# Token differences moved to VectorE in the first value group, two more dense units in the grouped-query stage, and earlier query and key loads in the dilated attention

## The chip, the cores and the metric

The kernel runs on one core of one Trainium2 chip. The metric is the device time of one execution, in microseconds (us); lower is better. A core has TensorE (PE in the profile, with its weight loads as PEld), VectorE (DVE), ScalarE (ACT), GpSimd (POOL) and SyncE (SP). Each works through its own queue in order, and they wait for one another and for transfers (DMA) by semaphores. Most transfers here are issued from SP's queue, some from ACT's. An issue that has to wait holds up everything behind it in that queue.

## The reference

One encoder block on a sequence of 1024 tokens with 1024 channels. A normalised input goes through one wide projection. Its columns feed three mixers: a dilated window attention of three groups (dilations 1, 4 and 16), a grouped-query attention of eight query heads on two key heads, and a cross-attention into 256 memory tokens. Each mixer has a gate path; each is projected back to 1024 channels, multiplied with a sigmoid gate of the merge columns (`mg`), summed, projected once more, normalised and added to the input.

```python
h = rms_norm(x, g_pre[layer])
a_qkv, bq, bk, bv, mq, ga, gb, gm, mg = jnp.split(h @ w_in[layer], split_at, axis=-1)
...
ya = (oa * jax.nn.silu(ga)) @ w_br_a[layer]
yb = (ob * jax.nn.silu(gb)) @ w_br_b[layer]
ym = (om * jax.nn.silu(gm)) @ w_br_m[layer]
gates = jax.nn.sigmoid((mg + b_merge[layer]).astype(jnp.float32)).astype(dt).reshape(b, s, N_BRANCHES, d)
merged = gates[:, :, 0] * ya + gates[:, :, 1] * yb + gates[:, :, 2] * ym
out = merged @ w_out[layer]
x = x + rms_norm(out, g_post[layer])
```

## The kernel before

**Precision.** A float32 operand is split into a high part (ACT copies it to the type fp32r, line 105) and a low part (DVE subtracts, line 106). A product takes three matmuls: high by high, low by high, high by low.

**Stages.** The work runs in this order, and the order of PE's instructions is written out by hand throughout.

1. Loading the input, the projection of the grouped keys and values, two gate units, the memory keys and values.
2. Cross-attention (`m_att`, line 589), woven by `weave` (line 174) with dense units: the query projections of the grouped-query attention (`b_q`, line 431), the cross-attention's query units (`mq_unit`) and one merge gate unit. A *dense unit* (`add_unit`, `add_filler`) is one 128-column slice of the big projection computed outright: two halves of 512 tokens, 24 matmuls each, so 48. A merge gate unit's result goes through DVE and ACT and is stored to the DRAM tensor `thd`.
3. Grouped-query attention (`b_att`, line 712), woven with the merge gate units of `FILL[1:]`.
4. Value groups (line 974 on): the projection of the dilated attention's values. The first group takes 16 steps (n = 0 to 15) of 12 matmuls and is a plain product. The other two groups are one matrix product in Winograd's form of Strassen's algorithm, with seven half-size products (28 steps).
5. Pairs (`order`, line 1199 on): the remaining projection units are taken two at a time in the same form: seven products of 12 matmuls, 84 for a pair. There are 5 gate pairs, 12 query-key pairs and 10 merge gate pairs.
6. Dilated attention, 12 items of four steps (`q` = 0 to 47), with the branch projections (`y_units`) as filler between them.
7. The rest of the branch projections, then the output projection.

**The token differences.** Strassen's form needs sums and differences of token blocks: of the scaled input x with channels in halves 1 and 2 and tokens in halves 1 and 2. `token_block(k)` (line 572) loads two rows of tiles of x, scales them on ACT (line 577) and returns four closures; each subtracts on POOL (line 583) and stores the result to the DRAM tensor `tsd` from SP's queue (line 584). `m_att(h)` calls `token_block(h)` in its first round and one closure in each of the next four. The value groups load `tsd` again from step n = 19 on (`blocks_at`), and the pairs do so as well (`t_load`).

**How weave sets the order.** `weave` alternates two generators, the dense units and the attention, so that both advance in proportion to their cost. A generator yields a cost per piece; the pads `START_PAD`, `END_PAD` and the six `yield 300` in `b_att` only shift where dense matmuls are put, and issue nothing. `B_COST` is the sum of the attention's costs.

**Queues.** From the value groups up to the last branch projections the order of ACT, DVE, POOL and SP is written out by hand too, so a line of the program that comes earlier is earlier in its engine's queue. In the stages before, a scheduler orders these four engines.

**The first value group's queues.** At n = 2 to 5 each step splits one quarter of `raw1` (the last weights of the group, steps 4 to 7) on ACT and DVE. From n = 14 on, `split_at` prepares the first product of the Strassen form, which starts at n = 16. At n = 8 to 11 and 16 to 19 ACT moves finished sums out of PSUM (`v_store`).

**The dilated attention's helpers.** In item n, at step j (n = q // 4, j = q % 4), `other(n, j)` runs after the filler of that step. For every third item it handles the weighting of the previous head pair: `fetch` at j = 0 (loads the statistics), `weights` at j = 1 (three DVE operations and an exponential on ACT), `weights2` and `load(0, 1)` at j = 2 (store the weights to DRAM, load them broadcast). At j = 2 it also issues the next item's values and `qk_load(n + 2)`:

```python
elif j == 2:
    COM[p_]["weights2"]()
    COM[p_]["load"](0, 1)
if j == 2:
    if n + 1 < len(items):
        items[n + 1]["values"]()
    if n + 2 < len(items):
        qk_load(n + 2)
```

Of the kernel before, what the change touches and what calls it, by code (L numbers as in the profile page):

```python
# [8 lines left out]
F32 = mybir.dt.float32  # L9
R = mybir.dt.float32r  # L10
AF = mybir.ActivationFunctionType
OP = mybir.AluOpType
# [38 lines left out]
def block(ctx: ExitStack, tc: tile.TileContext, x, xT, memT, cst, msk, bcst, tabA, gpost,  # L51
# [52 lines left out]
    def split(dst_h, dst_l, src):  # L104
        A.activation(dst_h, src, AF.Copy)  # L105
        V.tensor_tensor(dst_l, src, dst_h.bitcast(F32), op=OP.subtract)  # L106
# [462 lines left out]

    half = [slice(0, 512), slice(512, 1024)]  # L570

    def token_block(k):

        x1, x2 = [mt_.tile([P, S], F32, name=f"tx{j}", bufs=1) for j in range(2)]
        for j, t in enumerate((x1, x2)):
            nc.sync.dma_start(t, xT[k + 4 * j])
            A.activation(t, t, AF.Copy, scale=cs[:, C_GP + k + 4 * j:C_GP + k + 4 * j + 1])
        (b11, b12), (b21, b22) = [[t[:, h] for h in half] for t in (x1, x2)]
        T = [mt_.tile([P, 512], F32, name=f"tb{j}", bufs=1) for j in range(4)]

        def sub(j, x, y):
            def fn():
                G.tensor_tensor(T[j], x, y, op=OP.subtract)
                nc.sync.dma_start(tsd[j, k], T[j])
            return fn

        return [sub(0, b12, b11), sub(2, b22, b12), sub(1, b22, T[0]), sub(3, b21, T[1])]

    def m_att(h):
        qh, ql = MQ[h]  # L590
        for _ in range(4):
            yield 250
        st = {}

        def scores(n):
            sv = pss1().rearrange("p (t k) -> p t k", t=2)
            nm = mt_.tile([P, 2], F32, name="mnm", bufs=3)
            l = mt_.tile([P, 2], F32, name="mls", bufs=3)
            pm = mt_.tile([P, 2, 256], F32, name="pm", bufs=2)
            for j in range(2):  # L600
                t = slice((2 * n + j) * 128, (2 * n + j) * 128 + 128)
                passes(sv[:, j], [(qh[:, t], kmh[:, h]), (qh[:, t], kml[:, h]), (ql[:, t], kmh[:, h])])
            V.tensor_reduce(nm, sv, axis=AX.X, op=OP.min)
            V.tensor_tensor(nm, nm, rcol[:, 2 * n:2 * n + 2], op=OP.mult)
            for j in range(2):
                A.activation(pm[:, j], sv[:, j], AF.Exp, scale=nrcol[:, 2 * n + j:2 * n + j + 1], bias=nm[:, j:j + 1],
                             accum_out=l[:, j:j + 1])
            rl = mt_.tile([P, 2], F32, name="mrl", bufs=4)
            V.reciprocal(rl, l)
            for j in range(2):  # L610
                V.tensor_scalar(pm[:, j], pm[:, j], rl[:, j:j + 1], None, op0=OP.mult)
            st[n] = pm

        def trans(n):
            pm = st[n]
            tp = pst().rearrange("p (k t) q -> p k t q", k=2)
            for kt in range(2):
                for j in range(2):
                    PE.transpose(tp[:, kt, j, :], pm[:, j, kt * 128:kt * 128 + 128], ident)
            ph = mt_.tile([P, 2, 256], R, name="mph", bufs=2)  # L620
            pl = mt_.tile([P, 2, 256], R, name="mpl", bufs=2)
            split(ph, pl, tp.rearrange("p k t q -> p k (t q)"))
            st[n] = (ph, pl)

        def pv(n):
            ph, pl = st.pop(n)
            o = pso()
            terms = []
            for kt in range(2):
                terms += [(vmh[:, kt, h], ph[:, kt]), (vmh[:, kt, h], pl[:, kt]), (vml[:, kt, h], ph[:, kt])]  # L630
            passes(o[:, 0:256], terms)
            om = mt_.tile([P, 256], F32, name="om", bufs=2)
            A.activation(om, o[:, 0:256], AF.Copy)
            nc.sync.dma_start(od[2, h, :, n * 256:n * 256 + 256], om)

        for n in range(7):
            if n == 0:
                blocks = token_block(h)
            elif blocks:
                blocks.pop(0)()  # L640
            if n < 4:
                scores(n)
            yield 654
            if 0 <= n - 2 < 4:
                trans(n - 2)
            yield 436
            if 0 <= n - 3 < 4:
                pv(n - 3)
            yield 654
# [36 lines left out]
    with tc.tile_pool(name="ba", bufs=1, reuse_waits="tile") as ba:  # L686
# [25 lines left out]
        def b_att():  # L712
# [63 lines left out]
            q_prep(0)  # L776
            yield 436
            for _ in range(6):
                yield 300
            for n in range(128 + LAG_F + 8):  # L780
                if n < 128:
                    i, x = divmod(n, 8)
# [22 lines left out]
                    final(m // 8)  # L805
                    yield 432

        B_COST = 128 * 1080.0 + 16 * (218 + 432 + 109) + 1800 + LAG_T * START_PAD + (LAG_F + 8) * END_PAD
        for j in FILL[1:]:
            add_filler(j)  # L810
        early[len(queue)] = first_values
# [35 lines left out]
    raw1 = t23.tile([P, 4, 512], F32, name="sum1", tag="ac3")  # L847
    for i in range(2):
        nc.sync.dma_start(raw1[:, 2 * i:2 * i + 2], wv[VG[0], :, 4 + 2 * i:6 + 2 * i])
    VR = {}  # L850
    VT = {"A11": "ac0", "A21": "ac1", "A12": "ac2", "A22": "vA22"}
    for nm, u, kh in (("A21", 1, 0), ("A11", 0, 0), ("A22", 1, 1), ("A12", 0, 1)):
# [8 lines left out]
    def parts_of(t):  # L861
        return t[:, lo], t[:, hi]
# [113 lines left out]
    for n, (i, e, k) in enumerate(steps_v):  # L976
# [12 lines left out]
        if n + 2 < 8 and n + 2 >= 4:  # L989
            v_first.append(slots0[n - 2])  # L990
            split(*parts_of(v_first[-1]), raw1[:, n - 2])
        m = n + 2 - FIRST
        if 0 <= m < 28:
            split_at(*divmod(m, 4))
# [5 lines left out]
        for nm, s0 in (("S1", 7), ("S3", 11), ("S2", 17), ("S4", 21)):  # L1000
            if 0 <= n - s0 < 4:
                sum_at(nm, n - s0)
        if n == FIRST + 10:
            for j in range(2):
                nc.sync.dma_start(tab[j], tabA[:, j])
# [307 lines left out]
    for n, nm in order:  # L1313
# [14 lines left out]
            mask = aq.tile([P, 512], F32, name="mask")  # L1328
            nc.sync.dma_start(mask, msk)
        c = n - behind_qk  # L1330
        if nm == "1" and 0 < c < 9:
            operand_store()
        if nm == "4" and 0 <= c < 8:
            operand_load(2 - c // 4, c % 4)
# [21 lines left out]
    with tc.tile_pool(name="aa", bufs=1, reuse_waits="tile") as aa:  # L1356
# [247 lines left out]

        def other(n, j):
            p_, g = divmod(n, 3)
            if g == 0 and n:
                if j == 0:
                    COM[p_] = combine(p_ - 1)
                    COM[p_]["fetch"]()  # L1610
                elif j == 1:
                    COM[p_]["weights"]()
                elif j == 2:
                    COM[p_]["weights2"]()
                    COM[p_]["load"](0, 1)
            if j == 2:
                if n + 1 < len(items):
                    items[n + 1]["values"]()
                if n + 2 < len(items):
                    qk_load(n + 2)  # L1620
            if g == 1 and p_ and j:
                c = COM[p_]
                c["weigh"](j - 1)
# [72 lines left out]
        for q in range(NQS + 2):  # L1696
# [14 lines left out]
                items[q // 4 - 1]["stats"]()  # L1711
            if q % 2 and q > 2:
                items[(q - 2) // 4]["pv"]((q - 2) % 4 // 2)
            if it:
                fill(7 if q % 2 == 0 else 5)
                other(q // 4, j)
            elif q == NQS:
                lse_turn()
                e = last_weights()
                fill(12)  # L1720
# [106 lines left out]
    end_psum()  # L1827


START_PAD, END_PAD = 700, 300  # L1830
MN_A, MN_B = 0, 7
KV_K = 5
WR, KV_STEP, RB_WAIT, KN_PAD = 2, 700, 1500, 2800.0
# [3 lines left out]
G_AT = 4  # L1837
ATT_PRIO = 120
LA_T, LA_P = 2, 3
FILL = (16, 17, 18, 19)  # L1840
GATES = ((2, 2), (2, 3), (1, 0), (1, 1), (1, 2), (1, 3), (0, 0), (0, 1), (0, 2), (0, 3))
VG = (2, 0, 1)
Y_WOVEN = 12
# [108 lines left out]
```

## Time and profile before

| What | Value |
| --- | --- |
| Median of 3 runs | 1456.14 us (1455.86 to 1456.56) |
| Profiled execution, its own time | 1459.04 us |
| Its span, first to last instruction | 1457.2 us |
| ACT busy | 660.5 us (45%) |
| POOL busy | 568.9 us (39%) |
| DMA moved | 204.26 MB, mean 140 GB/s |
| Cross-attention woven with dense units | about 98 to 231 us |
| Grouped-query attention | about 231 to 443 us |
| Value groups | 443.4 to 563.4 us |
| Pairs | 563.4 to 1086.5 us |
| Dilated attention | 1086.5 to 1317 us |
| Branch rest and output | 1317 to 1457.2 us |

How to read it. A row of a timeline is: start, duration, engine, line of the program, operation, output <- inputs, shape and count, and in brackets the idle time of that engine just before it with what ended it. A row of a stage table is: from:to, length, then for PE, PEld, DVE, ACT and POOL the busy time with the count of instructions, the granted TensorE clock as a share of full speed, the busy share of the DMA engines and what they moved in GB/s. PE is nearly always busy by its records. But the record of a matmul is longer than the time from its start to the next one's start, since matmuls are pipelined, so its busy share hides short waits; the distance from start to start (the pitch) shows them. A row of the table of waits is: engine and line that waited, what it waited for, us in total, times, the longest.

### The profile page before, as it was taken

What the parts mean: (1) busy time and instruction counts of PE and PEld (TensorE: products, weight loads), DVE (VectorE), ACT (ScalarE), POOL (GpSimd) and SP (SyncE); (2) the same over time, 40 slices, a digit from 0 to 9 for tenths busy, and PEclk for the clock granted to TensorE, in tenths of its full rate; (3) what the DMA queues carried; (4) which work ended last, traced back from release to release, by engine and by line L of the source; (5) the groups of instructions that cost most, each with busy time, mean ns of one, the idle gap of its engine ahead of it and who ended that gap; (6) DMA issues with size and microseconds to landing.
All of it is one profiled execution on the core that took longest, in us unless ns stands there. A gap on an engine that the chain in (4) does not pass through costs nothing.

```text
span 1457.2 us, 21193 instructions
## 1 busy us (share of the span) xinstructions
PE 1410.4 (97%) x7535; PEld 1118.1 (77%) x7535; DVE 940.9 (65%) x1694; ACT 660.5 (45%) x1441; POOL 568.9 (39%) x457
## 2 busy tenths in 40 slices
PE   7997998999999999999999999999999999999998
PEld 7897886555557887888888888888887777777887
DVE  7764547776742377877887877556667656867543
ACT  6554344665652345433222222444447657632221
POOL 1429502767674202323455555223300012346422
PEclk9999999999999999999999999999999999999999
DMA  6364211010005263333556565656657467637222
GB/s 239 102 201 149 77 51 44 19 33 19 19 20 185 70 219 123 138 116 100 156 164 168 164 173 166 237 196 220 205 184 244 125 200 216 212 111 260 83 96 101
DMA packets 103466, 204.26 MB, mean 140 GB/s; under 512 B 19552, under 2 KB 49472, under 8 KB 103360
## 3 DMA queue, kind: packets, MB, share of 16 engines
q1 hardware_dynamic: 89008, 188.09, 40.9%
q10 hardware_dynamic: 14352, 14.81, 2.9%
q8 instruction: 59, 0.97, 0.3%
q14 instruction: 47, 0.39, 0.1%
HBM read 134.39 MB, written 55.89 MB: 131 GB/s over the span
## 4 chain that ended last, share of the span: by engine, by line
PE 74%; DVE 7%; issue 5%; DMA 5%; POOL 4%; ACT 3%; SPq 1%; ACTq 0%; POOLq 0%; DVEq 0%
PE s L1083 34%; PE d L1287 7%; PE s L987 6%; PE sc L1799 5%; PE ov L756 3%; PE d L1494 2%; PE d L987 2%; PE s L740 1%; PE s L1431 1%; DVE bn L723 1%; PE s L741 1%; DMA ak<-qkd 1%; PE d L145 1%; PE tr L722 1%; PE d L147 1%
## 5 line engine op out<-in xcount | busy, mean ns | idle before, releaser
L1083 PE MATMUL s<-T,ch 128*128 128x512 f32 x948 | 229.5, 395 | 0.0
L1083 PEld LDWEIGHTS s<-T,ch 128*128 128x128 f32 x948 | 177.8, 188 | 42.4 <-ACT sp L1148 0.3
L106 DVE TENSOR_TENSOR ch<-sf,ch 128x512 fp32r<-128x512 f32 x106 | 92.1, 875 | 78.3 <-ACT ch L105 78.3
L747 POOL TENSOR_TENSOR bl<-bl,bp 128x512 f32<-128x512 f32 x96 | 123.3, 1284 | 39.6 <-ACT bp L743 33.0
L1083 PE MATMUL s<-hh,ch 128*128 128x512 f32 x424 | 134.9, 389 | 0.0
L1287 PE MATMUL d<-hh,wh 128*128 128x512 f32 x384 | 126.6, 399 | 1.0 <-DVE wl L1293 1.0
L1083 PEld LDWEIGHTS s<-hh,ch 128*128 128x128 f32 x424 | 79.6, 188 | 16.5
L743 ACT ACTIVATE bp<-s 128x512 f32<-128x512 f32 x128 | 75.4, 594 | 36.3 <-PE s L741 33.6
L723 DVE TENSOR_REDUCE bn<-tr 128x1 f32<-128x512 f32 x128 | 84.0, 683 | 12.1 <-PE tr L722 11.4
L1148 ACT ACTIVATE sp<-s 128x512 f32<-128x512 f32 x54 | 32.2, 596 | 128.0 <-PE s L1083 106.7
L1116 POOL TENSOR_TENSOR o<-o,rc 128x1024 f32<-128x1024 f32 x24 | 61.6, 2565 | 72.0 <-DMA o<-rs 49.9
L1083 PE MATMUL s<-hh,wl 128*128 128x512 f32 x216 | 84.3, 390 | 1.6 <-DVE wl L106 1.6
L1294 POOL TENSOR_TENSOR acc<-acc,wl 128x512 f32<-128x512 f32 x32 | 57.8, 1808 | 71.1 <-DVE wl L1293 71.1
L1287 PEld LDWEIGHTS d<-hh,wh 128*128 128x128 f32 x384 | 72.0, 188 | 16.8 <-DVE wl L1293 1.6
L1083 PE MATMUL s<-hl,wh 128*128 128x512 f32 x216 | 84.3, 390 | 0.0
L1083 PE MATMUL s<-hh,wh 128*128 128x512 f32 x216 | 84.2, 390 | 0.0
L1083 PE MATMUL s<-hl,ch 128*128 128x512 f32 x212 | 82.5, 389 | 0.0
L105 ACT ACTIVATE wh<-wr 128x1024 fp32r<-128x1024 f32 (+1 forms) x63 | 55.1, 876 | 56.6 <-DMA wr<-in_wu 13.1
L965 POOL TENSOR_TENSOR sf<-wr,sf 128x512 f32<-128x512 f32 x27 | 35.7, 1324 | 111.0 <-DVE ch L106 111.0
L1449 ACT ACTIVATE pra<-pra,sts 128x192 f32<-128x192 f32 (+2 forms) x176 | 77.4, 442 | 2.2 <-DVE sts L1441 2.2
L1287 PE MATMUL d<-hl,wh 128*128 128x512 f32 x192 | 77.7, 405 | 0.0
L1589 POOL TENSOR_TENSOR og<-og 128x1024 f32<-128x1024 f32 (+1 forms) x9 | 18.4, 2051 | 144.2 <-DVE og L1586 141.9
(397 smaller groups left out, 3662.0 us busy)
## 6 DMA issues: line engine op xcount, KB each, us to landing
wr<-in_wu SPq DMA_DIRECT2D x38, 512.0 KB, 4.6
rw<-in_wu SPq DMA_DIRECT2D x26, 512.0 KB, 4.8
o<-rs SPq DMA_DIRECT2D x96, 128.0 KB, 2.3
qkd<-o SPq DMA_DIRECT2D x24, 512.0 KB, 3.3
wl<-thd SPq DMA_DIRECT2D x24, 512.0 KB, 7.1
thd<-rs ACTq DMA_DIRECT2D x40, 256.0 KB, 3.8
aq<-qkd SPq DMA_DIRECT2D x12, 512.0 KB
ak<-qkd SPq DMA_DIRECT2D x12, 512.0 KB, 6.4
```

The costliest lines, as they stand in the source:

```text
L105: A.activation(dst_h, src, AF.Copy)
L106: V.tensor_tensor(dst_l, src, dst_h.bitcast(F32), op=OP.subtract)
L723: fp["last"] = V.tensor_reduce(st[i]["n"][:, j, c:c + 1], s, axis=AX.X, op=OP.min)
L743: A.activation(pp, s, AF.Exp, scale=-1.0)
L747: G.tensor_tensor(lsum[i % 2], lsum[i % 2], pp, op=OP.add)
L987: PE.matmul(now[j], a, b, start=k == 0 and q == 0, stop=k == end and q == 2)
L1083: PE.matmul(dst, a, b, start=opens and i == 0, stop=closes and i == 11, skip_group_check=True)
L1116: G.tensor_tensor(QO[n, u], QO[n, u], RT.pop((n, u))[0], op=OP.add)
L1287: PE.matmul(s, a, b, start=q == 0, stop=q == 11)
L1294: G.tensor_tensor(accs[f][:, h], accs[f][:, h], th[:, h], op=OP.add)
L1449: A.activation(src, src, AF.Exp, scale=-1.0, bias=sums(T, h, 0), accum_out=sums(T, h, 1))
L1799: PE.matmul(parts[h], *terms[h][j], start=j == 0, stop=j == 23)
```

## The change

It has four parts.

1. **Token differences.** `token_block` and its calls leave the cross-attention. In the first value group, `x_load(k)` loads the two tiles of x into the two `wr` buffers, `x_scale(k)` scales them on ACT at n = 2, 6, 10 and 14, and `x_blocks(k)` subtracts on DVE and stores from SP at n = 3, 7, 11 and 15; the next `x_load` follows there.
2. **Dense units.** `FILL` grows from 4 to 6 units, so `FILL[1:]` in the grouped-query stage has five units in place of three, and the pairs lose one merge gate pair. The pads at the start of `b_att` grow.
3. **Last pair.** With one pair fewer, the eighth store of a gated operand (`operand_store`) goes to the last product.
4. **Dilated attention.** The next item's values and `qk_load(n + 2)` come ahead of `weights2` and `load(0, 1)`, and `weights` moves from the end of step j = 1 to the middle of step j = 2, ahead of that step's filler.

```diff
-    def token_block(k):
-        x1, x2 = [mt_.tile([P, S], F32, name=f"tx{j}", bufs=1) for j in range(2)]
-        for j, t in enumerate((x1, x2)):
-            nc.sync.dma_start(t, xT[k + 4 * j])
-            A.activation(t, t, AF.Copy, scale=cs[:, C_GP + k + 4 * j:C_GP + k + 4 * j + 1])
...
-                G.tensor_tensor(T[j], x, y, op=OP.subtract)
-                nc.sync.dma_start(tsd[j, k], T[j])
...
         for n in range(7):
-            if n == 0:
-                blocks = token_block(h)
-            elif blocks:
-                blocks.pop(0)()
...
             for _ in range(6):
-                yield 300
+                yield 1500
...
-        B_COST = 128 * 1080.0 + 16 * (218 + 432 + 109) + 1800 + LAG_T * START_PAD + (LAG_F + 8) * END_PAD
+        B_COST = 128 * 1080.0 + 16 * (218 + 432 + 109) + 9000 + LAG_T * START_PAD + (LAG_F + 8) * END_PAD
...
         nc.sync.dma_start(raw1[:, 2 * i:2 * i + 2], wv[VG[0], :, 4 + 2 * i:6 + 2 * i])
+    XT = []
+
+    def x_load(k):
+        XT[:] = [wp.tile([P, S], F32, name="wr", bufs=WR) for _ in range(2)]
+        for j, t in enumerate(XT):
+            nc.sync.dma_start(t, xT[k + 4 * j])
+
+    def x_scale(k):
+        for j, t in enumerate(XT):
+            A.activation(t, t, AF.Copy, scale=cs[:, C_GP + k + 4 * j:C_GP + k + 4 * j + 1])
+
+    def x_blocks(k):
+
+        (b11, b12), (b21, b22) = [[t[:, h] for h in half] for t in XT]
+        to = [(vv + vy)[(4 * k + j) % 8] for j in range(4)]
+        for j, x, y in ((0, b12, b11), (2, b22, b12), (1, b22, to[0]), (3, b21, to[1])):
+            V.tensor_tensor(to[j], x, y, op=OP.subtract)
+            nc.sync.dma_start(tsd[j, k], to[j])
+
+    x_load(0)
...
             split(*parts_of(v_first[-1]), raw1[:, n - 2])
+        if n < 16 and n % 4 == 2:
+            x_scale(n // 4)
...
+        if n < 16 and n % 4 == 3:
+            x_blocks(n // 4)
+            if n < 15:
+                x_load(n // 4 + 1)
...
-        if nm == "1" and 0 < c < 9:
+        if nm == "1" and 0 < c < 8 or (n, nm) == (last, "6"):
             operand_store()
...
         def other(n, j):
             p_, g = divmod(n, 3)
+            if j == 2:
+                if n + 2 < len(items):
+                    qk_load(n + 2)
+                if n + 1 < len(items):
+                    items[n + 1]["values"]()
             if g == 0 and n:
                 if j == 0:
                     COM[p_] = combine(p_ - 1)
                     COM[p_]["fetch"]()
-                elif j == 1:
-                    COM[p_]["weights"]()
                 elif j == 2:
                     COM[p_]["weights2"]()
                     COM[p_]["load"](0, 1)
-            if j == 2:
-                if n + 1 < len(items):
-                    items[n + 1]["values"]()
-                if n + 2 < len(items):
-                    qk_load(n + 2)
...
+            if j == 2 and q // 4 % 3 == 0 and 4 <= q < NQS:
+                COM[q // 12]["weights"]()
             if it:
                 fill(7 if q % 2 == 0 else 5)
                 other(q // 4, j)
...
-START_PAD, END_PAD = 700, 300
+START_PAD, END_PAD = 1400, 300
...
-FILL = (16, 17, 18, 19)
+FILL = (16, 17, 18, 19, 20, 21)
```

More of the change, by code (lines that the diff above doesn't have):

```diff
@@ L570, in block @@
     half = [slice(0, 512), slice(512, 1024)]
-    def token_block(k):
-        x1, x2 = [mt_.tile([P, S], F32, name=f"tx{j}", bufs=1) for j in range(2)]
-        for j, t in enumerate((x1, x2)):
-            nc.sync.dma_start(t, xT[k + 4 * j])
[L577 to L587, printed above, removed]
     def m_att(h):
```

## The prediction

> **What bounds the kernel now.** I read the page first, then the stage table, then each stage's waits and timelines.
>
> ```profile
> span 1457.2 us, 21193 instructions
> PE 1410.4 (97%) x7535; PEld 1118.1 (77%) x7535; DVE 940.9 (65%) x1694; ACT 660.5 (45%) x1441; POOL 568.9 (39%) x457
> ```
>
> PE's records cover 97% of the span, so the time is PE's work plus PE's waits. The chain of waits gives the pitch of matmuls in three stages:
>
> ```profile
> 253.61 3.58 PE ov L756 x16
> 507.67 1.36 PE d L987 x6
> 576.92 498.91 PE s L1083 x2170
> ```
>
> Divided by the counts: 0.224 us for a weighting matmul of the grouped-query stage, 0.227 for a 512-column one, 0.2299 averaged over the pairs, which run without a break. The stage table shows where there is slack:
>
> ```profile
> 98.00:152.00 54.00, 43.47 (x306) 40.30 (x305) 24.14 (x60) 21.49 (x44) 45.09 (x56) 0.97 0.51 173
> 160.00:170.00 10.00, 10.00 (x88) 10.00 (x86) 6.64 (x22) 3.55 (x11) 5.99 (x11) 1.00 0.01 2
> 233.50:443.40 209.90, 203.88 (x858) 117.62 (x858) 144.13 (x217) 124.05 (x216) 143.76 (x112) 1.00 0.08 25
> 443.40:563.40 120.00, 119.95 (x528) 99.13 (x529) 56.72 (x81) 45.12 (x77) 28.90 (x21) 1.00 0.50 161
> ```
>
> In the cross-attention, from 98 to 152 us, PE is without a matmul for 54.00 - 43.47 = 10.5 us, while POOL is at 45.09 of 54; at 160 to 170 PE has no gap. The value groups leave PE no gap, and DVE works there for 56.72 of 120 us.
>
> The sum is made against the profiled execution, 1459.04 us (span 1457.2 and 1.8 around it), which lies 2.9 above the median of 1456.14.
>
> **1. Token differences leave the cross-attention.** The change takes away 16 subtractions on POOL, 8 scalings on ACT and 24 issues in SP's queue.
>
> ```profile
> PE ov L125 <- ACT om L633: 6.2, 2, 3.8
> PE s L125 <- DVE t2b L326: 1.9, 1, 1.9
> PE s L125 <- ACT mqh L105: 2.7, 1, 2.7
> PE s L125 <- DVE mql L106: 0.9, 1, 0.9
>   DMA tx<-in_xT: 18.4, 5
> L583 POOL TENSOR_TENSOR tb<-tx,tb x8: 1260/1288/1297, 100.6 to 144.6; 128x512 f32<-128x512 f32 x8
> 132.15 11.04 SPq L584 DMA_DIRECT2D tsd<-tb  x5
> 146.35 0.88 SPq L114 DMA_DIRECT2D wr<-in_wu  x2
> ```
>
> These waits are 11.7 us of PE, and they have one root. A store of a difference waits in SP's queue for POOL (the five issues stretch over 11.04 us), and behind it stand the next loads of x and, at 146.35, weights. ACT then stands 18.4 us before scalings of x, with the eviction `om` and the query split `mqh` queued behind, and PE waits for those. After the gaps PE also runs slower for a while:
>
> ```profile
> 155.10 0.42 PE L307 MATMUL d<-wbl,hh 128*128 128x256 f32 x1
> 157.24 0.41 PE L303 MATMUL d<-wbh,hh 128*128 128x256 f32 x1
> 158.25 0.28 PE L307 MATMUL d<-wbl,hh 128*128 128x256 f32 x1
> 159.07 0.28 PE L303 MATMUL s<-wbh,hh 128*128 128x256 f32 x1
> ```
>
> The first two rows are ten matmuls apart, 0.214 us each; the last two seven apart, 0.117 each. That slow stretch has fifteen matmuls, 1.4 us lost; I take the same for the stretch that follows the 3.8 us wait. All in all up to 11.7 + 2.8 = 14.5 us. The other end is none, if other work waited as long. I take 12.5, near the upper end, since with the differences over, 160 to 170 us runs without a gap with the same projections and attention. What is late next is POOL's chain for the query norms, which that row has at 5.99 of 10 us.
>
> The Trainium skill (TensorE: Matmul & The Clock Gate, What's actually happening) has the array's clock drop to half after an idle window of about 3.4 us. No wait before the quoted stretch is that long (2.7 and 0.9 with work between), yet the pitch nearly doubles; counting only the 3.8 us wait by the rule, part 1 could bring 13.1 at most, so the rows stand.
>
> **2. Two units more beside the grouped-query attention.** One pair of 84 matmuls leaves the pairs: 84 x 0.2299 = 19.3 us less. Its loads, weight sums and evictions go with it, and the neighbouring pairs keep their own cover. Two units, 96 matmuls, come to the grouped-query stage: 96 x 0.227 = 21.8 us if nothing hides them.
>
> Its slack: by the program PE has there 559 matmuls of 512 columns (three for each of 128 steps, 143 dense, 32 sums) at 0.227, 256 at 0.224, and 76 small transposes, about 0.09 by their starts: 126.9 + 57.3 + 6.8 = 191 us, out of the 212 from 231.4 to 443.4. So 21 us are waits, and the growth lies between 0.8 (all filled) and 21.8 (none). Where they are:
>
> ```profile
> 231.40:244.00 12.60, 9.19 (x33) 4.50 (x32) 11.17 (x19) 3.35 (x7) 0.00 (x0) 1.00 0.22 73
> PE tr L722 <- ACT QH L700: 1.8, 1, 1.8
> 237.43 3.69 DVE bn L723 x6
> L756 PEld LDWEIGHTS ov<-bp,VS 128*64 128x64 f32 x256 | 17.0, 136 | 33.3 <-issue 33.3
> ```
>
> The start holds 33 matmuls in 12.6 us, 7.5 of work, so 5.1 are free: 1.8 is the wait for the first queries, and after it one DVE minimum of 0.615 us goes with each first score matmul. Just there the new pads put work. By the costs in the code, the attention's share up to the twelfth score matmul was (436 + 1800 + 12 x 916) / 167484 = 7.9%, beside 11 of 144 dense matmuls; it becomes (436 + 9000 + 12 x 1616) / 183084 = 15.7%, beside 38 of 240. So 27 new matmuls, 6.1 us, meet 5.1 free. The other 69, 15.6 us, go into the remaining 199 us, whose 16 us of waits are many of a few tenths; I let them take in 4.6. Growth: 1 + 11 = 12 us. DVE gets two units' work, about 5 us beside 144 in 210, so it does not come to bound.
>
> With the rule of the Trainium skill (Perfetto Trace Analysis, Identifying the Most-Contended Engine) that weight-load share, not matmul share, tells PE's headroom, this stage would have much: 117.62 of 209.90, beside 99.13 of 120 in the value groups. Against it stands the first row of the chain: those matmuls keep their 0.224 us though their weight load, 64 columns wide, takes 136 ns, so a low load share is no room.
>
> **3. Token differences in the first value group.** DVE does 16 subtractions, ACT 8 scalings, SP 8 loads and 16 stores, under 16 steps of 12 x 0.227 = 2.72 us. The prices:
>
> ```profile
> L584 SPq DMA_DIRECT2D tsd<-tb x16: 319/323/472, 99.1 to 145.9; - x16
> 443.94 0.69 DVE L106 TENSOR_TENSOR wh<-wr,wh 128x512 fp32r<-128x512 f32 x1
> 469.44 3.03 DVE L106 TENSOR_TENSOR sl<-vA,sl 128x512 fp32r<-128x512 f32 x3 [16.30 <-ACT sl L105]
> L577 ACT ACTIVATE tx<-tx,cs x8: 1142/1152/1156, 96.6 to 134.9; 128x1024 f32<-128x1024 f32 x8
> 447.12 0.85 SPq L855 DMA_DIRECT2D vA<-in_wv  x2
> 450.06 1.16 ACT L105 ACTIVATE sl<-sum 128x512 fp32r<-128x512 f32 x2 [3.97 <-DMA sum<-in_wv]
> DMA to landing us min/median/max: 4.0/4.0/4.0
> ```
>
> A subtraction is 0.69 us, or 1.0 beside POOL's sums: 2.8 to 4.0 for four. The last row is for the loads of x. Each `x_load` waits for the subtractions before it, as the buffers are two, so a round is 0.3 (store) + 0.8 (issues) + 4.0 + 1.15 + 2.8 to 4.0 = 9.1 to 10.3 us, and PE's four steps are 10.9. The first pair is issued where `vA` was and scaled by 447.1 + 0.45 + 4.0 + 1.15 = 452.7; the fourth by 480 to 484. Then `split_at` for step 16 follows on ACT (0.58, half the row at 450.06) and DVE (0.69), 1.3 us; that step starts at 443.4 + 16 x 2.72 = 487. Also behind the first scaling is the split of the weights of step 5, due at 457. So the work is covered with 2 to 6 us; should the second pair queue behind `vA` (eight loads of 512 KB), that is gone. `vA` itself lands later by two loads; its first split, the row at 469.44, ran 17 us ahead of step 16. A gain is excluded, as PE has no gap there. I take 1, up to 8.
>
> **4. Earlier queries and keys.**
>
> ```profile
> PE s L1431 <- DMA ak<-qkd: 4.9, 3, 3.2
> PE tr L1474 <- ACT app L1480: 2.1, 2, 1.3
> ACT ceg L1564 <- DVE ceg L1563: 9.4, 3, 3.9
> 1153.51 1.25 SPq L1576 DMA_DIRECT2D wgd<-ceg  x2
> 1156.11 2.40 SPq L1583 DMA_DIRECT2D wgt<-wgd  x4
> 1162.50 0.33 SPq L1170 DMA_DIRECT2D ak<-qkd  x1
> ```
>
> The keys are issued 9 us after the stores of weights and behind them. Ahead, they wait only for the score matmuls of their own step, and the three waits of 4.9 us go. The loads of weights (`wgt`) still wait for `wgd`, which DVE's `weights2` sets as before; the seven issues now ahead of them fit into SP's wait for it. `weights` moves behind the next step's masks, so its statistics have landed; ACT's 9.4 us in front of `ceg`, with the exponentials behind, should shrink, and with it PE's 2.1 for `app`. Together 7.0; I take 6.5. Ends: 0, if DVE's weighting of `og` is late instead, to 14.3, if all of 4.9 and 9.4 were on the path. The last pair's later store delays a load needed three steps afterwards: nothing.
>
> **Sum.** -12.5 - 19.3 + 12 + 1 - 6.5 = -25.3 us: 1433.7 as the profiled execution, 1430.8 as the median; I say 1431.
>
> **The rivals.** (a) *The cross-attention keeps other waits.* Its norms and evictions also cross ACT, DVE and POOL, and the scheduler reorders them. Part 1 then brings 5: 1438.5. Against it: the row at 160. (b) *The new loads fill SP for nothing in the dilated attention*: `wgt` lands late, DVE holds the masks, part 4 brings 0: 1437.5. (c) *The grouped-query stage has room*, so the units cost 1 and not 12: 1420. That is what the skill's rule on weight loads would make of it; the pitch speaks against it. (d) *Slower: the chain of x loads.* In the first value group ACT stands at `x_scale(3)` with the first Strassen split behind it, and PE stops at step 16. PE waits as soon as the three rounds after 452.7 end past about 485.7, 11 us each. To eat the 26 us that the rest brings, they would need 20 us each, so loads landing in 14 us instead of 4.0; 1460 at 21 us each. For it: the DMA engines are taken up by `vA` then. Against it: those loads all end in the first rounds.
>
> **How the numbers follow.** Forecast 0.70, (a) 0.12, (b) 0.07, (c) 0.08, (d) 0.03. The range 1421 to 1442 takes in (a), (b), nearly (c), and the unknown costs within a few us of their values (up to 8 in part 3, 4 either way in part 2). About 0.2%, 2.9 us, is what a measurement of this kernel can tell from no change: faster 0.96, same 0.01, slower 0.03.
>
> **What would show it.** Right: from 98 to 184 us PE without gaps over 1 us and at 0.117 us pitch; the stage from q_prep to the value groups about 224 us; 26 pairs in place of 27 at the same pitch; no `ak` wait at line 1431; at most 1 to 2 us of PE wait around step 16 of the value groups. Wrong: waits for `om` or `mqh` that stay, a grouped-query stage over 232 us, a PE wait for an `sl` split in the value groups, or `wgt` named as what DVE waits for.

## The result and the profile after

| | Before | After |
| --- | --- | --- |
| Median | 1456.35 us (1455.86 to 1456.85, 4 runs) | 1437.2 us (1435.49 to 1439.32, 4 runs) |
| Ratio, 95% interval | | 0.9869 [0.9852, 0.9886] |
| Profiled execution, span | 1459.04, 1457.2 us | 1437.71, 1435.9 us |

The change brought 19 us by the medians, 21.3 by the two spans; 25.3 had been forecast. The stages show where it came from and where some of it went. Each length is measured from the first matmul of a stage to the first of the next (from `q_prep`'s first transpose on, since the cross-attention's end is woven); the differences are those of the unrounded lengths.

| Length in us | Before | After | Difference | Forecast |
| --- | --- | --- | --- | --- |
| start to `q_prep` | 231.0 | 214.9 | -16.1 | -12.5 |
| `q_prep` to value groups | 212.5 | 222.5 | +10.1 | +12 |
| value groups | 120.1 | 129.6 | +9.5 | +1 |
| pairs, to the first A score | 526.3 | 507.2 | -19.0 | -19.3 |
| dilated attention and branch rest | 273.8 | 268.0 | -5.8 | -6.5 |
| output projection | 87.2 | 87.2 | 0 | 0 |

Four terms stand within 4 us of their forecast. The value groups don't. First the page of after, then its stage table (columns as in the table of before):

```profile
span 1435.9 us, 21185 instructions
PE 1405.6 (98%) x7547; PEld 1121.0 (78%) x7547; DVE 949.7 (66%) x1703; ACT 658.3 (46%) x1434; POOL 546.7 (38%) x437
```

```profile
98.00:152.00 54.00, 54.00 (x418) 52.07 (x418) 31.49 (x87) 21.18 (x54) 32.85 (x55) 1.00 0.16 52
228.00:437.40 209.40, 207.75 (x903) 128.19 (x902) 140.39 (x207) 128.11 (x218) 144.39 (x112) 1.00 0.10 32
437.40:567.10 129.70, 123.33 (x530) 100.89 (x530) 75.17 (x97) 53.88 (x86) 33.61 (x21) 0.97 0.64 214
```

In the first row PE works through: 418 matmuls in the 54 us in which there were 306 before, and POOL is at 32.85 in place of 45.09. The last row is new: before, PE had 119.95 of 120 us there; now 6.4 us are without a matmul, and the granted clock is 0.97. The table of waits names one place for it, and three short stretches, the wait and what comes behind it, show the rest:

```profile
PE s L986 <- DVE sl L106: 6.4, 2, 6.2
```

```profile
455.00:460.00 5.00, 0.00 (x0) 0.00 (x0) 3.13 (x4) 0.00 (x0) 1.77 (x2) 0.94 1.03 417
460.00:465.00 5.00, 4.42 (x10) 3.48 (x11) 2.21 (x2) 0.00 (x0) 5.00 (x4) 0.50 0.97 384
465.00:470.00 5.00, 5.00 (x21) 4.04 (x20) 2.54 (x3) 3.57 (x4) 5.00 (x4) 0.88 0.26 96
```

PE waits 6.2 us ahead of step 6 of the first value group, then runs at a clock of 0.50 and 0.88, which costs at most 5 x 0.50 + 5 x 0.12 = 3.1 us (the first of these windows begins with 0.6 us without a matmul). Together that is up to 9.3 of the 9.5 us. The Trainium skill (TensorE: Matmul & The Clock Gate, What's actually happening) has the clock fall to half after an idle window of about 3.4 us; this wait and the 0.50 behind it agree.

What PE waited for is seen in DVE's and SP's timelines (start, duration, engine, line, operation):

```profile
451.15 0.68 DVE L845 TENSOR_TENSOR vv<-wr 128x512 f32<-128x512 f32 x1
456.84 0.69 DVE L845 TENSOR_TENSOR vv<-wr 128x512 f32<-128x512 f32 x1 [5.00 <-DMA thd<-fth]
457.45 1.41 DVE L845 TENSOR_TENSOR vv<-wr,vv 128x512 f32<-128x512 f32 x2
458.78 3.43 DVE L106 TENSOR_TENSOR sl<-sum,sl 128x512 fp32r<-128x512 f32 x2
```

```profile
445.53 1.85 SPq L854 DMA_DIRECT2D vA<-in_wv  x4
447.48 0.45 SPq L214 DMA_DIRECT2D thd<-fth  x1
```

The second subtraction of `x_blocks(0)` stands for 5 us, and the split of the weights behind it on DVE (458.78) comes late. It waits for a store of a merge gate unit (`thd<-fth`). That its target, the third `vv` tile, lies on the memory of that unit's `fth` is inferred from this wait; the store had been issued only at 447.48, behind four loads of `vA`. So the first theory was: *this store's memory costs the 9 us.* The rival was rival (d) of the prediction in kind: *the chain of x loads through ACT is too slow for the stage*, and what stands at step 6 only shifts that.

### The profile page after: what moved, and what is told of

The parts are those of the page before. It is cut to its first block, busy times and chain, and to the rows that moved or that the text cites. A ratio compares the mean times of both kernels' runs of the same rounds, so it can differ in the third digit from the quotient of the medians.

```text
span 1435.9 us, 21185 instructions
## 1 busy us (share of the span) xinstructions
PE 1405.6 (98%) x7547; PEld 1121.0 (78%) x7547; DVE 949.7 (66%) x1703; ACT 658.3 (46%) x1434; POOL 546.7 (38%) x437
## 4 chain that ended last, share of the span: by engine, by line
PE 77%; DMA 5%; DVE 5%; issue 5%; ACT 3%; POOL 2%; SPq 1%; ACTq 0%; DVEq 0%; POOLq 0%
PE s L1088 30%; PE d L1292 9%; PE sc L1804 5%; PE ov L735 4%; PE s L1436 3%; PE d L1499 3%; PE d L143 3%; PE d L147 2%; PE d L145 2%; PE s L719 2%; PE tr L701 2%; PE s L720 2%; DMA or<-rld 2%; PE d L536 2%; PE tr L1479 1%
## 5 line engine op out<-in xcount | busy, mean ns | idle before, releaser
L1088 PE MATMUL s<-T,ch 128*128 128x512 f32 x912 | 220.8, 395 | 0.0
L1088 PEld LDWEIGHTS s<-T,ch 128*128 128x128 f32 x912 | 171.1, 188 | 40.8 <-ACT sp L1153 0.3
L1088 PE MATMUL s<-hh,ch 128*128 128x512 f32 x408 | 129.9, 389 | 0.0
L1292 PE MATMUL d<-hh,wh 128*128 128x512 f32 x384 | 126.6, 398 | 1.1 <-DVE wl L1298 1.0
L1088 PEld LDWEIGHTS s<-hh,ch 128*128 128x128 f32 x408 | 76.6, 188 | 15.9
L1088 PE MATMUL s<-hh,wl 128*128 128x512 f32 x208 | 81.2, 391 | 1.6 <-DVE wl L106 1.6
L1088 PE MATMUL s<-hl,wh 128*128 128x512 f32 x208 | 81.2, 390 | 0.0
L1088 PE MATMUL s<-hh,wh 128*128 128x512 f32 x208 | 81.1, 390 | 0.0
L1088 PE MATMUL s<-hl,ch 128*128 128x512 f32 x204 | 79.4, 389 | 0.0
L143 PE MATMUL d<-hh,wh 128*128 128x512 f32 x192 | 76.5, 399 | 1.7 <-DVE fth L222 1.7
L147 PE MATMUL d<-hh,wl 128*128 128x512 f32 x192 | 76.5, 398 | 0.0
```

Of the source, the lines that this page charges most:

```text
L143: PE.matmul(dst, wh[:, k, :], hh[k][:, t], start=k == 0, stop=False)
L147: PE.matmul(dst, wl[:, k, :], hh[k][:, t], start=False, stop=k == 7)
L1088: PE.matmul(dst, a, b, start=opens and i == 0, stop=closes and i == 11, skip_group_check=True)
L1292: PE.matmul(s, a, b, start=q == 0, stop=q == 11)
```

## The experiments

All ratios are to the kernel before, run on the same chip, with the 95% interval.

**e1_after_splits and e2_other_tiles: two ways around the store.** The first moves `x_blocks(0)` behind the splits of steps 4 to 7, the second gives it the other tiles first.

```diff
-        if n < 16 and n % 4 == 3:
-            x_blocks(n // 4)
+        if n in (5, 7, 11, 15):
+            x_blocks((n - 3) // 4)
             if n < 15:
-                x_load(n // 4 + 1)
+                x_load((n - 3) // 4 + 1)
```

> Theory: the 6.2 us for which PE stands still in the first value group of the changed kernel come from the order in DVE's queue. The four subtractions of the first round stand ahead of the split of the weights of step 6, and one of them waits 5.0 us for the store of the last dense unit's result, whose memory its target tile takes over. With the first round put two steps later, behind the splits, that wait no longer has PE behind it: value groups 120 to 122 us instead of 129.4, about 1429 us. Rival 1: the chain of x loads is the cause; then the wait moves to step 16, where the first Strassen splits stand behind the last round, 3 to 6 us there, about 1434 us. Rival 2: the DMA engines are overloaded by x beside the values' weights, and the splits themselves are late: value groups stay above 127 us.

```diff
-        to = [(vv + vy)[(4 * k + j) % 8] for j in range(4)]
+        to = [(vy + vv)[(4 * k + j) % 8] for j in range(4)]
```

> Theory: only the target tile matters. The first round writes to the other four tiles, which no store of the stage before holds; order and loads are as in the changed kernel. DVE's wait for the store of the dense unit goes, the split of step 6 is ready about 1 us after PE wants it, value groups 120 to 122 us, about 1429 us. Rivals: if the loads of x or the place of the subtractions in DVE's queue are the cause, PE stands still as long as in the changed kernel, value groups about 129 us, 1437 us; the same if the other tiles also lie on memory that is still being stored.

Measured: 1439.13 us, 0.9881 [0.9857, 0.9906], and 1439.44 us, 0.988 [0.9859, 0.99]; value groups 129.6 and 130.6 us. Nothing gained. PE's waits in the value groups, of e1 and of e2:

```profile
PE s L986 <- ACT sl L105: 7.7, 1, 7.7
```

```profile
PE s L986 <- ACT sl L105: 7.8, 1, 7.8
```

The wait at step 6 is gone in both, and a wait of 7.7 and 7.8 us stands at step 16 (from 480.67 to 488.77 in e1), now for ACT. The kernel of e7 below, whose value groups have the code of after unchanged, shows the same: there no subtraction waits for the store, step 6 is free, and step 16 waits.

```profile
PE s L986 <- ACT sl L105: 8.7, 1, 8.7
```

So the store was the place of the wait and not its limit. Without it the loss comes ten steps later, at the same size.

**e3_store_earlier: the last operand's store.** At the start of the dilated attention, PE waits in after where it did not before. PE's, ACT's and SP's rows of after:

```profile
1098.06 1.54 PE L1470 MATMUL tr<-cs,pra 128*128 128x128 f32 x6 [2.40 <-ACT app L1485]
```

```profile
1094.72 1.06 ACT L105 ACTIVATE hh<-ot 128x1024 fp32r<-128x1024 f32 x1 [3.46 <-DMA ot<-od]
```

```profile
1062.21 8.01 SPq L1263 DMA_DIRECT2D wr<-in_wbr  x2
1070.31 0.38 SPq L1269 DMA_DIRECT2D wl<-thd  x1
1070.79 0.40 SPq L1195 DMA_DIRECT2D od<-aq  x1
1076.54 0.32 SPq L1175 DMA_DIRECT2D aq<-qkd  x1
```

The eighth store of a gated operand (`od<-aq`) stands in SP's queue behind two loads of branch weights that stretch over 8.01 us. The next queries take the tile that it frees, so they are issued at 1076.54, and the split of the operand on ACT is late, with the exponentials queued behind it. The edit issues the store one product earlier (the last pair's products run in the order 4, 3, 7, 5, 2, 6):

```diff
-        if nm == "1" and 0 < c < 8 or (n, nm) == (last, "6"):
+        if nm == "1" and 0 < c < 8 or (n, nm) == (last, "2"):
```

> Theory: in the changed kernel the last gated operand's store stands in SP's queue behind a load that waits for a buffer, and the load of the second item's queries waits for that store to land (5.3 us on SP); the loads of the grouped-query result behind it come late, ACT stands before them and PE waits 2.4 us and more at about 1098 us. With the store one product earlier, ahead of that load, the dilated attention is 3 to 5 us shorter (from the last pair to the output projection 267 to 269 us instead of 271.7), about 1433 us. Rival: those loads are late because the DMA engines are full then; the store's place changes nothing, 1437 us.

Measured: 1435.22 us, 0.9854 [0.9836, 0.9872]; from the first A score to the output 265.2 us in place of 268.0; value groups 130.9. SP's rows of e3:

```profile
1067.52 0.33 SPq L1195 DMA_DIRECT2D od<-aq  x1
...
1072.55 0.41 SPq L1175 DMA_DIRECT2D aq<-qkd  x1
```

The queries go 4 us sooner, and PE's wait shrinks from 2.4 to 0.6 us. The medians alone couldn't tell these 2 us, as the intervals overlap. The stage can, since the four kernels with the early store (e3, e4, e10, e13) give 264.8 to 265.6 us there, and the five with the late one and the same code (after, e1, e2, e5, e7) 266.6 to 269.7.

**e4_both: all three edits.**

> The three edits together: first round of subtractions behind the splits and in the other tiles, the last store one product earlier. If the theories hold they add, since the places are 600 us apart: 8 to 9 and 3 to 5 us less than the changed kernel, 1424 to 1427 us, a ratio to the kernel before of 0.978 to 0.980. If one falls, 1428 to 1434 us.

Measured: 1435.78 us, 0.9858 [0.9841, 0.9875]; value groups 130.2. PE's wait, and ACT's rows of e4 that lead to it:

```profile
PE s L986 <- ACT sl L105: 8.2, 1, 8.2
```

```profile
446.30 2.42 ACT L838 ACTIVATE wr<-wr,cs 128x1024 f32<-128x1024 f32 x2 [7.01 <-DMA wr<-in_xT]
464.65 2.41 ACT L838 ACTIVATE wr<-wr,cs 128x1024 f32<-128x1024 f32 x2 [14.37 <-DMA wr<-in_xT]
475.18 2.42 ACT L838 ACTIVATE wr<-wr,cs 128x1024 f32<-128x1024 f32 x2 [6.37 <-DMA wr<-in_xT]
485.91 2.39 ACT L838 ACTIVATE wr<-wr,cs 128x1024 f32<-128x1024 f32 x2 [6.57 <-DMA wr<-in_xT]
488.21 1.65 ACT L105 ACTIVATE sl<-vA 128x512 fp32r<-128x512 f32 x3
```

These are the four scalings of x and, right behind the fourth, the first Strassen split. The rounds take 18.4, 10.5 and 10.7 us; the split could have run at 480, but ACT stands 6.57 us for the fourth pair of x in front of it. Why the first round is long is seen in SP's rows of e4:

```profile
451.82 4.34 SPq L846 DMA_DIRECT2D tsd<-vy  x4
457.06 1.61 SPq L834 DMA_DIRECT2D wr<-in_xT  x2
466.56 3.35 SPq L846 DMA_DIRECT2D tsd<-vv  x4
470.00 1.99 SPq L834 DMA_DIRECT2D wr<-in_xT  x2
```

The stores of the first round stretch over 4.34 us. That isn't their own time, as each issue takes 0.33 us, nor DVE's, which has subtracted for the fourth time at 453.70, 2.1 us before the last store is issued. SP's table of waits from 440 to 492 us names what they and the two loads behind them wait for:

```profile
SPq L846 <- DMA vA<-in_wv: 4.3, 4, 1.7
SPq L834 <- DMA vA<-in_wv: 1.7, 2, 0.9
```

By this table they wait until loads of `vA` have landed. The second pair is issued at 457.06 and scaled 7.6 us later, the third 5.2 us after its issue. In after, the rows from 455 to 465 have the DMA engines at 1.03 and 0.97 of their time.

**e10_last_later: the fourth round behind the first Strassen splits.** If ACT's order is the limit, the fourth scaling only has to go behind the splits that it blocks; its result is read back at step 22.

```diff
-        if n < 16 and n % 4 == 2:
-            x_scale(n // 4)
+        if n in (2, 6, 10, 18):
+            x_scale(min(n // 4, 3))
...
-        if n in (5, 7, 11, 15):
-            x_blocks((n - 3) // 4)
-            if n < 15:
-                x_load((n - 3) // 4 + 1)
+        if n in (5, 7, 11, 19):
+            k_x = min((n - 3) // 4, 3)
+            x_blocks(k_x)
+            if k_x < 3:
+                x_load(k_x + 1)
...
-        to = [(vy + vv)[(4 * k + j) % 8] for j in range(4)]
+        to = vv if k == 1 else vy
```

> All of e4_both, and beside it the fourth round of the token differences later: x_scale(3) at n = 18 and x_blocks(3) at n = 19, behind the splits of the first Strassen product (its output goes to the tiles vy, so that A11's sums find vv free). Theory (the scaling of the fourth pair on ACT stands ahead of the first Strassen splits, and that alone is what still costs the value groups about 9 us): no PE gap at step 6 nor at step 16, value groups 121 +- 1 us in place of 130.2, output behind the first A score 265, time 1426.5. Rival (the two loads of a round and their stores are too slow for the stage wherever they stand): the wait moves on to step 20 to 24, where the last differences are read back; value groups 127 to 131, time 1433 to 1436.

Measured: 1426.73 us (1425.19 to 1428.73), 0.9807 [0.9792, 0.9821]; value groups 120.7 us, and no PE wait in them is left. The stage row and ACT's rows of e10:

```profile
437.40:558.00 120.60, 120.60 (x529) 98.79 (x528) 70.23 (x97) 53.55 (x86) 30.42 (x21) 1.00 0.69 230
```

```profile
480.46 1.68 ACT L105 ACTIVATE sl<-vA 128x512 fp32r<-128x512 f32 x3 [0.44 <-ACT vr L903]
...
487.04 1.15 ACT L838 ACTIVATE wr<-wr,cs 128x1024 f32<-128x1024 f32 x1 [2.67 <-DMA wr<-in_xT]
```

The split runs at 480.46 and the scaling behind it, waiting 2.67 us for x at no cost. The DMA share is higher than in after (0.69), and DVE and ACT do the same work. So neither the transfers nor the engines were too slow for the stage: one instruction stood in front of another in ACT's queue. My first theory falls. Of the rival, the place holds (the chain of x loads ends too late for step 16), but not that the chain is too slow for the stage. e10 contains the edits of e1 and e2 as well; no run moves the fourth scaling alone, and by the rows of after the wait of 6.2 us at step 6 would then be left.

**e5_blocks_back: part 1 undone.** `token_block` and its calls are put back, `x_load`, `x_scale` and `x_blocks` are left out.

> After, with part 1 undone: the token differences are back in the cross-attention (POOL subtracts, SP's queue stores), none in the first value group; the other three parts stay. Theory (part 1 alone makes both the gain before the first query norm and the loss in the value groups): q_prep at 231 us in place of 214.9 (+16), value groups back to 120 (-9.5), dilated attention up to output unchanged at 268: time 1437.2 + 6.5 = 1443.7. Rival (the cross-attention gained because the scheduler reorders with the new costs of the other parts, not because the differences left): q_prep at 218 to 224, time 1431 to 1436.

Measured: 1446.19 us, 0.9938 [0.9923, 0.9953]; `q_prep` at 231.4 us, value groups 120.0. Both the gain and the loss are part 1's, and they come and go together: 16.5 us against 9.6 by the profiles, whose spans differ by 6.6 (the medians by 9.0).

**e6_pool_queue_stores and e6_dve_blocks: which root.** The prediction gave the cross-attention's waits one root: SP's queue, where a store that waits for POOL holds up loads. Two edits of one word each in the kernel before ask whether it is the queue or POOL.

```diff
-                nc.sync.dma_start(tsd[j, k], T[j])
+                nc.gpsimd.dma_start(tsd[j, k], T[j])
```

> The kernel before, with one word changed: the 16 stores of token differences in the cross-attention are issued from POOL's own queue in place of SP's. Theory (one root: a store that waits for POOL holds up the loads of x and of weights behind it in SP's queue, and everything late follows from that): ACT's 18.4 us in front of the scalings of x shrink to under 8, PE's waits for om and mqh (11.7 us with the two on DVE) to under 4; q_prep at 219 to 223 in place of 231.0, time 1444 to 1448. Rival (POOL is simply too slow with 16 subtractions of 1.29 us more, whoever issues the stores): the waits stay, q_prep 229 to 232, time 1454 to 1457.

```diff
-                G.tensor_tensor(T[j], x, y, op=OP.subtract)
+                V.tensor_tensor(T[j], x, y, op=OP.subtract)
```

> The kernel before, with the 16 subtractions of the cross-attention on DVE in place of POOL; the stores stay in SP's queue. Theory of the queue: the stores wait less since DVE subtracts sooner and in 0.7 to 0.9 us, so part of the waits goes: q_prep at 222 to 228, time 1447 to 1452. Rival (POOL's time is the root): nearly all of them go, q_prep at 215 to 219, time 1440 to 1444.

Measured: with POOL's queue 1460.37 us, 1.0029 [1.0016, 1.0042], `q_prep` at 234.0; with DVE 1440.53 us, 0.9894 [0.9876, 0.9912], `q_prep` at 216.1. From 98 to 152 us, the first and the second:

```profile
98.00:152.00 54.00, 40.61 (x274) 37.97 (x273) 23.27 (x60) 21.80 (x45) 49.85 (x65) 0.87 0.51 162
```

```profile
98.00:152.00 54.00, 53.71 (x412) 51.41 (x411) 42.02 (x103) 26.87 (x58) 35.67 (x54) 1.00 0.56 193
```

Taking the stores out of SP's queue made it worse; taking POOL out recovered 14.9 of the 16.1 us, though stores and loads stay in SP's queue. SP's waits of the first show why the queue alone is no test: the next loads of x still wait for POOL, which reads the tiles.

```profile
SPq L576 <- POOL tb L583: 29.7, 5, 9.3
```

So the subtractions' time on POOL is the root. How much of it spreads through SP's queue stays open: with DVE, SP's waits at these stores fell too (from 31.6 to 13.8 us), and no run takes the stores out of SP's queue without loading POOL with them. The row of the subtractions of e6_dve_blocks, to be held against the 1288 ns on POOL in the prediction:

```profile
L583 DVE TENSOR_TENSOR tb<-tx,tb x8: 675/684/1108, 99.9 to 133.0; 128x512 f32<-128x512 f32 x8
```

**e7_old_pads and e13_wider_pads: where the dense matmuls stand.** e7 puts the old pads back (300, 1800, 700); e13 widens them in e10 (3000, 18000, 2100).

> After, with the three old numbers that place the dense matmuls of the grouped-query stage (the six pads of 300, 1800 in B_COST, START_PAD 700); the five units stay. Theory (the new pads put 27 more matmuls where the first scores wait for queries, and these 6 us are hidden but for about 1): from q_prep to the value groups 227 us in place of 222.6, time 1441 to 1442. Rival (where the dense matmuls stand doesn't matter, the first scores aren't bound by what these hide): 222 to 223.5, time 1437 +- 1.

> e10_last_later with more of the dense matmuls at the start of the grouped-query stage: the six pads 3000 and START_PAD 2100, which by the costs puts some 17 more before the first weighting. Theory (the 38 matmuls there already fill what was free): what they take there they save later, 222.5 +- 1 us from q_prep to the value groups, time 1426 to 1428. Rival (the waits at the start still have room, as 26 matmuls there hid 4.9 us): 3 us more are hidden, 219.5 us, time 1423.5.

Measured: e7 1443.99 us, 0.992 [0.9903, 0.9936], 227.5 us from `q_prep` to the value groups; e13 1425.85 us, 0.9791 [0.9772, 0.9811], 222.4 us. The old pads cost 5.0 us (PE's wait for the first queries is back, at 1.3 us, with some tenths for each minimum); wider ones bring no more. e13 and e10 can't be told apart.

**e11_keys_behind and e12_weights_back: the halves of part 4.** e11 issues keys, queries and values behind `weights2` and `load(0, 1)` again; e12 puts `weights` back at the end of step j = 1.

```diff
-            if j == 2:
-                if n + 2 < len(items):
-                    qk_load(n + 2)
-                if n + 1 < len(items):
-                    items[n + 1]["values"]()
...
+            if j == 2:
+                if n + 1 < len(items):
+                    items[n + 1]["values"]()
+                if n + 2 < len(items):
+                    qk_load(n + 2)
```

> After, with the queries, keys and values of the next items issued behind the weights again (as before); the weights' own computation stays at its new place. Theory (two separate halves: the order of the issues is worth the 4.9 us of the three waits for keys): those waits come back, first A score to output 272.5 in place of 268.0, time 1441.7; ACT's wait in front of ceg stays at about 3. Rival (the early weights do it all: with them the stores go sooner, and the keys behind them land in time): 268 to 269, time 1437 to 1438.

```diff
+                elif j == 1:
+                    COM[p_]["weights"]()
...
-            if j == 2 and q // 4 % 3 == 0 and 4 <= q < NQS:
-                COM[q // 12]["weights"]()
```

> After, with the weights' computation back at the end of step j = 1; the queries, keys and values stay issued ahead of the weights' stores. Theory (the two halves of part 4 add up): ACT waits about 9 us in front of ceg again in place of 3, 1 to 2 of it reach PE, first A score to output 269 to 270 in place of 268.0, time 1438 to 1439. Rival (the place of the weights doesn't matter, part 4 is the order of the issues alone): 268.0 +- 0.4, time 1437.

Measured: e11 1441.93 us, 0.9912 [0.9898, 0.9927], 272.1 us from the first A score to the output; e12 1439.49 us, 0.9888 [0.987, 0.9906], 270.2 us. PE's wait in e11 and ACT's in e12, then ACT's in after:

```profile
PE s L1436 <- DMA ak<-qkd: 2.4, 2, 1.8
```

```profile
ACT ceg L1569 <- DVE ceg L1568: 7.7, 3, 3.3
```

```profile
ACT ceg L1569 <- DVE ceg L1568: 3.0, 2, 1.6
```

Each wait comes back in part or nearly whole with its half (2.4 of the 4.9 us for keys, 7.7 of ACT's 9.4). For e11 the time says the same (its interval lies above that of after); for e12 the intervals overlap and 270.2 lies only 0.5 us outside the 266.6 to 269.7 of unchanged code, so its 2 us are likely, not shown.

## Why the prediction was right, and where not

The time of 1437.2 us lies in the range, 6 us above the 1431 forecast. The sign and the mechanisms held; one term was mis-sized by 8.5 us, of which part 1 gave back 3.6 and part 2 1.9; that the total lies so near is in part luck. (These are of the two profiled executions; their difference, 21.3, is 2 us more than that of the medians.)

**Part 3, the token differences in the value group: the step that failed.** It was put at +1 us, up to 8, "covered with 2 to 6 us". It is +9.5. The working allowed the three rounds after the first scaling 485.7 - 452.7 = 33 us and put them at 27.3 to 30.9. With the store's memory out of the way (e4) they take 39.6. Rounds two and three are nearly as costed (10.5 and 10.7 beside 9.1 to 10.3). The first takes 18.4. From the end of one scaling to the end of the next it is, in e4: 2.4 us until DVE begins to subtract, with splits of weights ahead of it (nothing had been counted); 2.6 for the subtractions (2.8 to 4.0); 3.4 until the second pair's first load is issued, as SP waits for loads of `vA` to land (0.3); 7.6 from there to the scaling (4.8 for issues and landing); and 2.4 for the two scalings (1.15). The 3.4 and the 7.6 are what the working names, the second pair behind `vA`, and then sets aside. The first scaling also ends 2.4 us later in the stage than the working had it (448.72 - 437.02 = 11.7 us beside 452.7 - 443.4 = 9.3). Rival (d) was this mechanism, at its place (step 16) and with its rule: 39.6 - 33 = 6.6 us of wait, which in place of the 1 gives 1436.6. That this is so near to 1437.2 is chance in part, since in after PE waits at step 6. The prediction's own sign of being wrong, a PE wait for an `sl` split in the value groups, is there in after and in e4. The rival was set aside as too small to turn the sign, which was right, and priced as if it came at full size or not at all, which was not; and its argument against, that the loads of `vA` end in the first rounds, overlooked that the first round is where the chain is lost. The slow clock behind the wait (3.1 us in after) was in no term, though the prediction had read just that in the cross-attention. Not foreseen at all was the other form of the wait, a target tile on memory with a pending store.

**Part 1: right, larger.** -16.1 where 12.5 was taken and 14.5 was the bound. PE runs without gaps from 98 us on, as foretold. The bound was low, but not by the slow matmuls that the working put at 2.8 us. By the granted clock of before they cost:

```profile
135.00:140.00 5.00, 1.91 (x8) 1.81 (x9) 3.42 (x7) 4.16 (x7) 4.72 (x6) 0.77 0.58 214
140.00:145.00 5.00, 5.00 (x21) 4.13 (x20) 1.12 (x1) 0.21 (x1) 4.64 (x7) 0.89 0.23 82
...
150.00:155.00 5.00, 1.96 (x13) 1.75 (x14) 3.33 (x4) 2.98 (x5) 0.00 (x0) 0.97 0.46 162
155.00:160.00 5.00, 5.00 (x32) 5.00 (x32) 3.01 (x11) 1.97 (x6) 2.93 (x5) 0.68 0.44 159
```

At most 5 x (0.23 + 0.11 + 0.03 + 0.32) = 3.5 us, as the first of these windows is partly without a matmul. By the starts of the matmuls the two stretches lost 1.5 and 1.4 us, so the 2.8 was right. What was low are the waits, since the table of waits counts from the end of a matmul's record and not from where the next could have started:

```profile
133.93 0.39 PE L147 MATMUL d<-hh,wl 128*128 128x512 f32 x1
138.09 0.58 PE L125 MATMUL ov<-mph,vmh 128*128 128x256 f32 x1 [3.78 <-ACT om L633]
```

These starts are 4.16 us apart where 0.23 is the pitch of such a matmul: 3.93 lost, not 3.78. By the starts the five waits come to 12.4 us, and 12.4 + 2.9 = 15.3; the rest, 0.8, lies in steps of under 0.3 us each and stays open. That the subtractions on POOL are the root, the prediction had half: it named the store that waits for POOL, and what has to go are POOL's 16 x 1.29 us, which DVE does in 0.69 each.

**Part 2: right.** +10.1 beside 12; the pair 19.0 beside 19.3; the pads hid 5.0 where 5.1 was worked out. The stage is PE-bound as its pitch said: rival (c), that low weight-load share means room, would have had +1.

**Part 4: right in sum, by two errors.** The forecast was -6.5, with "nothing" for the last pair's later store. That store costs 2.8 us (e3), so the rest brought 8.6 in this pair of profiles. This stage varies: the three profiles that have the code of before give 269.4, 273.0 and 273.8 us, so of the 5.8 us some 2 may be chance. No wait for keys is left.

**What it adds to.** With the value groups free of waits and the store earlier, e10 takes 1426.73 us, 4 below the forecast. A shorter way may be e6_dve_blocks' single word together with parts 2 and 4: it leaves the value groups untouched and has `q_prep` only 1.2 us later. That combination was not run.

## What to carry to other kernels

When work is moved into a stage where an engine is half idle, follow its longest chain (load, scale, subtract, store, next load into the same two buffers) round by round against the first deadline behind it in each queue; busy shares say nothing of that, and the first round, in the transfers of the stage change, is the one to price highest. When such a chain is late, move the instruction that waits behind the ones that don't (9 us from e4 to e10) before making the chain faster. And before moving work to another stage, try it on another engine where it is: here one word brought 15.5 us.

## What was not expected of the hardware

A store issued from POOL's queue costs POOL time. The row of these issues in e6_pool_queue_stores (its columns are duration in ns, min/median/max, and the first and last start):

```profile
L584 POOL DMA_DIRECT2D tsd<-tb x16: 539/622/788, 100.1 to 153.6; - x16
```

The same sixteen issues took a median of 323 ns on SP in before. On POOL they are 16 x 0.62 = 10 us of an engine that was busy for 45.09 of 54 us already, which fits that the edit ended 0.3% slower. The slow clock in before also came late: the waits of 2.7 and 0.9 us end at 153.55, matmuls from there to 154.7 run at full pitch, and the drop (0.68) falls into 155 to 160. By the Trainium skill's rule quoted above neither wait alone is long enough; no run here separates whether the two count together.
